# A Mamba-2 scan inside a transformer layer: outputs for pairs of chunks, and the state update beside its own chunk

## The chip, the cores and the metric

The kernel runs on one core of a Trainium2 chip. The metric is the device time of one execution in microseconds (us): the median of three runs before the change is 2607.29 us (2604.95 to 2607.7). The engines that matter are TensorE (PE: matmuls and transposes; its weight loads are listed as PEld), VectorE (DVE), ScalarE (ACT), GpSimd (POOL) and SyncE (SP, which issues most DMAs). Each works through its own instructions in the order in which they stand in the program, and waits on semaphores for the others.

## What is computed

One decoder layer on 1024 tokens of width 1024, in float32: a SwiGLU half, a mixer, a cross-attention to 256 memory tokens, a second SwiGLU half, each with an RMSNorm before and after. The mixer projects the tokens once and gives half of the heads to a stick-breaking attention and half to a Mamba-2 SSD. The change touches the SSD alone. Its core in the reference, cut:

```python
x = xs * dt[..., None]                      # (chunk, 128 tokens, 16 heads, 64)
a_cs = cumsum(dt * a)                       # along the 128 tokens of a chunk
lmat = exp(where(tri, a_cs[l] - a_cs[s], -inf))
cb = einsum('bclgn,bcsgn->bcgls', cc, bc)   # C times B, per group of 8 heads
y_diag = einsum('bcgls,bgrcls,bcsgrp->bclgrp', cb, lmat, x)
states = einsum('bclgn,bgrcl,bclgrp->bcgrpn', bc, exp(a_cs[-1] - a_cs), x)
h = h * exp(a_cs[-1]) + states              # scan over the 8 chunks
y_off = einsum('bclgn,bcgrpn,bgrcl->bclgrp', cc, h_before, exp(a_cs))
y = y_diag + y_off + d_skip * xs            # then gated by silu(z) and normed
```

## The kernel before

Every large product is made of three float32r matmuls on high and low parts of the operands (`mm3`, L275). The work of TensorE is written in one fixed order: each matmul or transpose is chained to the one before it (`_pe`, L101), and so the Python code decides what stands behind what. VectorE and ScalarE get their order from the tile framework's scheduler when the program is built; it is as fixed when the program runs.

The SSD (`ssd`, L1208) runs two generators side by side. `inproj` (L1525) is the filling work: the input projections of the remaining x, B, C and z tiles, three 128x512 matmuls to a step, then the keys of the cross-attention (`keys`, L1498, with 128x256 matmuls). `chunks` (L1419) is the scan. It goes over four quads of four heads, and in each over eight chunks of 128 tokens. `merge` (L157) alternates between the two by the matmul costs that each has used, in the ratio 89000 to 149000; a step of the scan ends at each `yield`.

For a chunk, `early` (L1343) makes what needs no state. On TensorE these are a matmul for the differences of the decay sums (tile `seg`), from the second chunk of a quad on another for the decays from the chunk's start (also a `seg` buffer), and two transposes of x (tile `ms`). ScalarE makes `L` of the first by a Relu (L1356) and an Exp (L1357), and `E` of the second by an Exp (L1364). VectorE makes `xdt` (x times dt, L1371), `M` (L times C B, L1376), `E` times C (L1381) and `xdec` (xdt times the last column of L, L1386). `chunk` (L1391) then has the state matmul (tile `st`, of `xdec`, L1398), the new state `S` on VectorE (L1403, L1406), and eight matmuls into `y` that use 64 columns of the array: four on `M` and, from the second chunk on, four on `S` and `E`. In float32 each of these passes twice, so the profile counts 16. VectorE adds `y` to the skip term (L1413). The loop calls `early` for chunk n+1 and only then `chunk` for chunk n (L1429). `bc` (L1332) makes the C B products and the transposed B, one chunk at a call.

When a quad is done and its z tile exists, `gates` (L1449) multiplies by silu(z), stores the result and adds up squares; `group_norm` (L1475) makes the norm's factors. Behind the merge stand the last gates, the last two keys and the last group norm (L1590 to L1594), then the attention. Silu and Exp do not share a table of ScalarE's, so a table load stands in the program wherever it goes from one to the other.

Of the kernel before, what the change touches and what calls it, by code (L numbers as in the profile page):

```python
# [18 lines left out]
P = 128  # L19
S = 1024  # L20
# [27 lines left out]
class Kern:  # L48
# [1159 lines left out]
    def ssd(self, close):  # L1208

        nc, ap = self.nc, self.ap  # L1210
        with self.tc.tile_pool(name=self.nm("ssa"), bufs=1, reuse_waits="tile") as ep, \
# [120 lines left out]
            def bc(gr, c):  # L1332

                Bt, Ct = env["bc", gr]
                _, cbm, Bl = env["g", gr]
                cs = slice(c * P, (c + 1) * P)
                ps = self.t(pp, [P, 2, P], F32, "seg", bufs=2)
                self.mm(ps[:, 0, :], Bt[:, cs], Ct[:, cs], True, True)
                self.tr(ps[:, 1, :], Bt[:, cs])
                nc.vector.tensor_tensor(out=cbm[:, c, :], in0=ps[:, 0, :], in1=self.tri, op=ALU.mult)  # L1340
                nc.scalar.copy(Bl[:, c, :], ps[:, 1, :])

            def early(qd, c):  # L1343
                hs = slice(4 * qd, 4 * qd + 4)
                xs, (Ct, cbm, Bl), (dt, row, col) = env["x", qd], env["g", qd // 2], env["dt"]

                rb = self.t(sp, [P, 4, P], F32R, "rb", bufs=2)
                nc.vector.tensor_tensor(
                    out=rb, in0=row[:, c, :].bitcast(F32).unsqueeze(1).to_broadcast([P, 4, P]),
                    in1=self.par("sel", 6 + 4 * qd, 4).unsqueeze(2).to_broadcast([P, 4, P]), op=ALU.mult,  # L1350
                )
                seg = self.t(pp, [P, 4, P], F32, "seg", bufs=2)
                self.mm(seg, col[:, c, :], rb, True, True)
                L = self.t(sp, [P, 4, P], F32, "L", bufs=2)

                nc.scalar.activation(L, seg, AF.Relu, scale=-1.0)  # L1356
                nc.scalar.activation(L, L, AF.Exp, scale=-1.0)  # L1357
                E = ed = None
                if c > 0:
                    es = self.t(pp, [P, 4, P], F32, "seg", bufs=2)  # L1360
                    self.mm(es, side, rb, True, True)
                    E = self.t(sp, [P, 4, P], F32, "E", bufs=2)
                    ed = self.t(sp, [P, 4, 1], F32, "ed", bufs=2)
                    nc.scalar.activation(E, es, AF.Exp)  # L1364
# [5 lines left out]
                xdt = self.t(sp, [P, 4, 64], F32, "xdt", bufs=2)  # L1370
# [5 lines left out]
                nc.vector.tensor_tensor(  # L1376
                    out=M, in0=L, in1=cbm[:, c, :].unsqueeze(1).to_broadcast([P, 4, P]), op=ALU.mult
                )
                xdec = None
                if c > 0:  # L1380
                    nc.vector.tensor_tensor(  # L1381
                        out=E, in0=E, in1=Ct[:, cs].unsqueeze(1).to_broadcast([P, 4, P]), op=ALU.mult
                    )
                if c < 7:
                    xdec = self.t(sp, [P, 4, 64], F32, "xdec", bufs=2)
                    nc.vector.tensor_tensor(  # L1386
                        out=xdec, in0=xdt, in1=L[:, :, P - 1 : P].to_broadcast([P, 4, 64]), op=ALU.mult
                    )
                return ed, xdt, M, E, xdec

            def chunk(qd, c, St, ed, xdt, M, CE, xdec):  # L1391
                xs, Bl = env["x", qd], env["g", qd // 2][2]
                cs = slice(c * P, (c + 1) * P)
                yp = self.t(pp, [P, 2, P], F32, "y", bufs=1)
                Sn = None
                if c < 7:
                    sps = self.t(pp, [P, 4, 64], F32, "st", bufs=1)
                    self.mm(sps, Bl[:, c, :], xdec, True, True)  # L1398
                    Sn = self.t(sp, [P, 4, 64], F32, "S", bufs=2)
                    if St is None:  # L1400
                        nc.vector.tensor_copy(Sn, sps)
                    else:
                        nc.vector.tensor_tensor(  # L1403
                            out=Sn, in0=St, in1=ed.to_broadcast([P, 4, 64]), op=ALU.mult
                        )
                        nc.vector.tensor_tensor(out=Sn, in0=Sn, in1=sps, op=ALU.add)  # L1406
                for h in range(4):
                    o = yp[(h % 2) * 64 : (h % 2) * 64 + 64, h // 2, :]
                    self.mm(o, xdt[:, h, :], M[:, h, :], True, St is None)
                    if St is not None:  # L1410
                        self.mm(o, St[:, h, :], CE[:, h, :], False, True)
                for i in range(2):
                    nc.vector.scalar_tensor_tensor(  # L1413
                        out=xs[i][:, cs], in0=xs[i][:, cs], scalar=self.par("d_skip", 2 * qd + i),
                        in1=yp[:, i, :], op0=ALU.mult, op1=ALU.add,
                    )
                return Sn

            def chunks():  # L1419
                env["dt"] = dt_sums(*dt_wide)  # L1420
                yield
                env["g", 0] = env["bc", 0][1], self.t(sp, [P, 8, P], F32, "cbm"), self.t(sp, [P, 8, P], F32, "Bl")
                bc(0, 0)
                yield
                order = [(n // 8, n % 8) for n in range(32)]
                nxt = early(*order[0])
                bc(0, 1)
                yield
                for n, (qd, c) in enumerate(order):  # L1429
                    cur, nxt = nxt, None  # L1430
                    if n < 31:
                        nxt = early(*order[n + 1])
                    St = chunk(qd, c, None if c == 0 else St, *cur)
                    if c == 7:
                        ready.append(qd)
                    gates()
                    if n < 6:
                        bc(0, n + 2)
                    yield
                    if qd == 1 and c > 3:  # L1440

                        env["g", 1] = env["bc", 1][1], *env["g", 0][1:]
                        for i in range(2):
                            bc(1, 2 * (c - 4) + i)
                        yield
# [74 lines left out]
            env = {}  # L1520
# [35 lines left out]
            for i, ti in enumerate((8, 10, 0, 1)):  # L1556
                ps = self.proj_now(next(W), 1)
                if i == 0:
# [6 lines left out]
                    sp = late.enter_context(self.tc.tile_pool(name=self.nm("ssb"), bufs=1, reuse_waits="tile", side="right"))  # L1565
                    pp = late.enter_context(self.tc.tile_pool(name=self.nm("ssps"), bufs=1, reuse_waits="tile", space=PSUM))
# [15 lines left out]
            fill = inproj()  # L1582

            scan = chunks()
            for n in (4, 2, 7):
                for _ in range(n):
                    next(fill)
                if n < 7:
# [807 lines left out]
```

## Time and profile before

| | |
|---|---|
| median of 3 runs | 2607.29 us |
| the profiled execution, span from the first to the last instruction | 2606.7 us |
| busy share: TensorE, weight loads, VectorE, ScalarE, GpSimd | 99%, 82%, 76%, 49%, 22% |
| the scan's matmuls: first seg, last y | 755.5 us, 991.5 us |
| y matmuls (M and S together) | 480 passes, median 0.27 us each as recorded |
| st matmuls | 56 passes for 28 chunks, median 0.38 us as recorded |

The median of the runs is 0.6 us above the profiled execution's span; nothing else lies around it. A matmul's recorded length includes the time in which the next one already streams, so a sum of lengths says little; the distance from one start to the next tells what a matmul costs. In a profile row, `out<-in` are the program's tile names, a number in brackets at the end is idle time before the instruction, with what ended it, and `L1386` is a line of the kernel.

### The profile page before, as it was taken

The numbers are of one execution on the slowest core, as the hardware profiler recorded it, in microseconds if no ns is written. First come the engines' busy times: TensorE is split into PE (matmuls) and PEld (weight loads), VectorE is DVE, ScalarE is ACT, GpSimd is POOL, SyncE is SP. The second block draws the span as 40 slices with busy tenths as digits, with TensorE's granted clock in tenths as the row PEclk, the third lists the DMA queues.
The fourth block names the chain that finished last, engine by engine and source line by source line (L and its number), as shares of the span: only waits on it lengthen the run. The fifth ranks groups of instructions, "written<-read, shape, count | busy, mean of one in ns | idle before, by whom it ended". The sixth has DMA issues, their size and how long they took to land.

```text
span 2606.7 us, 36814 instructions
## 1 busy us (share of the span) xinstructions
PE 2578.2 (99%) x12850; PEld 2148.5 (82%) x12850; DVE 1993.9 (76%) x3044; ACT 1289.7 (49%) x2300; POOL 577.9 (22%) x669
## 2 busy tenths in 40 slices
PE   9999999999999999999999999999999999999999
PEld 7788888888777778888888898888878888888887
DVE  7978987779689884777777777876656888777767
ACT  7434444555356663555555554445554433334543
POOL 2655554001000001111111110101011655551000
PEclk9999999999999999999999999999999999999999
DMA  6468887655656516555555556547558453326554
GB/s 241 158 210 298 300 287 272 209 188 169 224 195 204 182 69 213 162 149 152 141 152 131 169 161 215 206 153 250 196 185 299 146 183 104 109 85 236 184 174 154
DMA packets 216042, 489.82 MB, mean 188 GB/s; under 512 B 26544, under 2 KB 35120, under 8 KB 215856
## 3 DMA queue, kind: packets, MB, share of 16 engines
q1 hardware_dynamic: 169232, 381.02, 44.6%
q0 software_dynamic: 22720, 62.93, 8.1%
q10 hardware_dynamic: 23904, 43.53, 4.5%
q8 instruction: 101, 1.65, 0.3%
q14 instruction: 85, 0.70, 0.1%
HBM read 327.46 MB, written 138.94 MB: 179 GB/s over the span
## 4 chain that ended last, share of the span: by engine, by line
PE 77%; issue 13%; DVE 5%; ACT 1%; DMA 1%; POOL 0%; DVEq 0%; ACTq 0%; POOLq 0%
PE mm L139 38%; PE dn L139 34%; PE z L139 2%; PE tr L142 2%; PE ms L139 1%; PE ms L142 1%; DVE nb L1770 1%; DVE wlo L263 0%; DVE acc L363 0%; DVE hl L263 0%; DVE atl L263 0%; DVE F L1053 0%; DVE xl L263 0%; DVE F L405 0%; DVE xl L417 0%
## 5 line engine op out<-in xcount | busy, mean ns | idle before, releaser
L139 PE MATMUL mm<-xh,whi 128*128 128x512 f32 x1320 | 520.3, 403 | 2.5 <-ACT xh L268 1.1
L139 PE MATMUL mm<-xh,wlo 128*128 128x512 f32 x1272 | 488.7, 391 | 0.0
L139 PE MATMUL mm<-xl,whi 128*128 128x512 f32 (+1 forms) x1252 | 486.9, 389 | 1.8 <-DVE xl L263 1.4
L139 PEld LDWEIGHTS mm<-xh,whi 128*128 128x128 f32 x1320 | 248.2, 188 | 44.6 <-issue 3.8
L139 PEld LDWEIGHTS mm<-xh,wlo 128*128 128x128 f32 x1272 | 238.8, 188 | 52.1 <-DVE wlo L263 0.4
L139 PEld LDWEIGHTS mm<-xl,whi 128*128 128x128 f32 x1252 | 236.1, 189 | 35.9 <-DVE xl L263 2.3
L1770 DVE TENSOR_TENSOR_SCAN nb<-nb,begin 128x128 f32<-128x128 f32 (+7 forms) x128 | 171.3, 1351 | 50.8 <-ACT nb L1766 49.8
L1766 ACT ACTIVATE nb<-z,scale 128x128 f32<-128x128 f32 (+2 forms) x192 | 107.8, 581 | 78.8 <-PE z L139 78.6
L263 DVE TENSOR_TENSOR wlo<-wraw,whi 128x1024 fp32r<-128x1024 f32 x70 | 85.5, 1222 | 54.3 <-ACT whi L261 54.0
L261 ACT CAST whi<-wraw 128x1024 fp32r<-128x1024 f32 (+1 forms) x87 | 84.0, 965 | 78.3 <-PE mm L139 51.1
L658 ACT ACTIVATE ft<-ft 128x512 f32<-128x512 f32 x88 | 55.5, 631 | 99.3 <-DVE ft L657 97.3
L1787 POOL DMA_DIRECT2D mix<-sq x64 | 52.8, 826 | 231.0 <-DVE sq L1785 168.0
L139 PE MATMUL dn<-xh,wlo 128*128 128x512 f32 x296 | 101.3, 390 | 0.0
L757 POOL TENSOR_TENSOR wc<-raw,wraw 128x512 f32<-128x512 f32 x55 | 81.2, 1476 | 57.7 <-DVE blk L263 24.8
L263 DVE TENSOR_TENSOR atl<-tr,ath 128x512 fp32r<-128x512 f32 (+1 forms) x108 | 67.9, 632 | 31.2 <-ACT ath L261 30.8
L757 POOL TENSOR_TENSOR wc<-wraw,raw 128x512 f32<-128x512 f32 x56 | 80.2, 1432 | 50.9 <-DVE whi L263 16.6
L844 POOL TENSOR_TENSOR ft<-ft,e 128x512 f32<-128x512 f32 x37 | 59.7, 1614 | 121.2 <-DVE e L843 45.8
L139 PE MATMUL mm<-ath,v 128*128 128x256 f32 x320 | 85.9, 291 | 0.8 <-ACT sq L1784 0.6
L261 ACT CAST ath<-tr 128x512 fp32r<-128x512 f32 (+1 forms) x108 | 58.9, 546 | 53.3 <-PE tr L142 48.9
L139 PE MATMUL dn<-xh,blk 128*128 128x512 f32 x264 | 85.1, 389 | 0.0
L261 ACT CAST wlo<-wc 128x512 fp32r<-128x512 f32 x79 | 49.1, 621 | 69.9 <-PE dn L139 23.2
L139 PE MATMUL mm<-atl,v 128*128 128x256 f32 x320 | 82.8, 281 | 0.7 <-DVE atl L263 0.7
(579 smaller groups left out, 6775.6 us busy)
## 6 DMA issues: line engine op xcount, KB each, us to landing
whi<-dwhi SPq DMA_DIRECT2D x82, 512.0 KB, 3.6
wlo<-dwlo SPq DMA_DIRECT2D x82, 512.0 KB, 4.7
wraw<-in_w_gu SPq DMA_DIRECT2D x43, 512.0 KB, 4.0
dwhi<-bh SPq DMA_DIRECT2D x78, 256.0 KB, 4.1
dwlo<-bl SPq DMA_DIRECT2D x78, 256.0 KB, 3.9
raw<-in_w_gu SPq DMA_DIRECT2D x37, 512.0 KB, 4.0
wraw<-xs SPq DMA_DIRECT2D x56, 256.0 KB, 3.0
xs<-ft ACTq DMA_DIRECT2D x54, 256.0 KB, 3.7
```

Source lines behind the costliest of these rows:

```text
L139: self._pe(self.nc.tensor.matmul(out, lhsT, rhs, start=start, stop=stop, skip_group_check=self.more), cost)
L142: self._pe(self.nc.tensor.transpose(out, src, self.ident if ident is None else ident), 109.0)
L261: self.kp(self.nc.scalar.copy(hi, src))
L263: self.nc.vector.tensor_tensor(out=lo, in0=src, in1=hi.bitcast(F32), op=ALU.subtract)
L658: nc.scalar.activation(t, t, AF.Silu)
L757: inst = nc.gpsimd.tensor_tensor(out=t, in0=a, in1=b, op=op)
L844: nc.gpsimd.tensor_tensor(out=t1, in0=t1, in1=e, op=ALU.mult)
L1766: nc.scalar.activation(nb[:, s0:s1], z[:, 0:n], AF.Sigmoid, scale=sc[:, i : i + 1])
L1770: nc.vector.tensor_tensor_scan(out=nb[:, 0:Wd][:, ::-1], data0=nb[:, 0:Wd][:, ::-1], data1=begin[:, S - Wd : S][:, ::-1], initial=0.0, op0 ...
L1787: nc.gpsimd.dma_start(out=self.mix_d[p][a * 64 : a * 64 + 64, csl], in_=o, accum_op=ALU.add)
```

## The change

- `early` writes `M` into `L`'s buffer and `E` into one of `rb`'s (both "in place"), makes `xdec` ahead of `M`, and the buffer counts are changed to suit: rb 4, L 3, ed 3, xdt 3, S 3; M and E have no buffers of their own any more.
- `chunk` is split into `state` (the st matmul and the new S) and `outputs` (the y matmuls and the skip term). The loop takes two chunks at a time: `early`, `state`, `early`, `state`, then `outputs` for both, into one `y` tile, with two VectorE instructions on 256 columns instead of four on 128. A `yield` stands between each of these, so that filling work goes there. The call of `early` one chunk ahead is gone.
- `bc` calls are spread over the new steps.
- Eleven steps of projections, not seven, stand ahead of the first chunk.
- The last keys stand ahead of the last gates, and the last group norm's matmuls are pinned 12000 cost units into the attention.

```diff
-                rb = self.t(sp, [P, 4, P], F32R, "rb", bufs=2)
+                rb = self.t(sp, [P, 4, P], F32R, "rb", bufs=4)
...
-                    E = self.t(sp, [P, 4, P], F32, "E", bufs=2)
+                    E = self.t(sp, [P, 4, P], F32, "rb", bufs=4)
...
-                M = self.t(sp, [P, 4, P], F32, "M", bufs=2)
-                nc.vector.tensor_tensor(
-                    out=M, in0=L, in1=cbm[:, c, :].unsqueeze(1).to_broadcast([P, 4, P]), op=ALU.mult
-                )
...
                     xdec = self.t(sp, [P, 4, 64], F32, "xdec", bufs=2)
                     nc.vector.tensor_tensor(
                         out=xdec, in0=xdt, in1=L[:, :, P - 1 : P].to_broadcast([P, 4, 64]), op=ALU.mult
                     )
+                M = L
+                nc.vector.tensor_tensor(
+                    out=M, in0=L, in1=cbm[:, c, :].unsqueeze(1).to_broadcast([P, 4, P]), op=ALU.mult
+                )
...
-            def chunk(qd, c, St, ed, xdt, M, CE, xdec):
...
+            def state(qd, c, St, ed, xdec):
+                if c == 7:
+                    return None
+                Bl = env["g", qd // 2][2]
+                sps = self.t(pp, [P, 4, 64], F32, "st", bufs=1)
+                self.mm(sps, Bl[:, c, :], xdec, True, True)
...
+            def outputs(qd, c, parts):
+
+                xs = env["x", qd]
+                yp = self.t(pp, [P, 2, 2, P], F32, "y", bufs=1)
+                for j, (St, xdt, M, CE) in enumerate(parts):
+                    for h in range(4):
+                        o = yp[(h % 2) * 64 : (h % 2) * 64 + 64, h // 2, j, :]
+                        self.mm(o, xdt[:, h, :], M[:, h, :], True, St is None)
+                        if St is not None:
+                            self.mm(o, St[:, h, :], CE[:, h, :], False, True)
...
-                for n, (qd, c) in enumerate(order):
-                    cur, nxt = nxt, None
-                    if n < 31:
-                        nxt = early(*order[n + 1])
-                    St = chunk(qd, c, None if c == 0 else St, *cur)
...
+                for n in range(16):
+                    qd, c = n // 4, n % 4 * 2
+                    if c == 0:
+                        St = None
+                    parts = []
+                    for j in range(2):
+                        ed, xdt, M, CE, xdec = early(qd, c + j)
+                        if n == 0:
+                            bc(0, 1 + j)
+                        yield
+                        Sn = state(qd, c + j, St, ed, xdec)
+                        parts.append((St, xdt, M, CE))
+                        St = Sn
+                        if n < 3 and 3 + 2 * n + j < 8:
+                            bc(0, 3 + 2 * n + j)
+                        yield
+                    outputs(qd, c, parts)
+                    if c == 6 and qd < 3:
                         ready.append(qd)
                     gates()
...
-            for n in (4, 2, 7):
+            for n in (4, 2, 11):
...
             self.merge(scan, 89000, fill, 149000)
+            self.run_all(keys(6, 8))
             gates()
-            self.run_all(keys(6, 8))
             self.run_later(float("inf"))
-            group_norm(1)
+            with self.pinned(self.clock + 12000):
+                group_norm(1)
```

What this does to the order on TensorE is best seen at one chunk of the first quad. Before, from the last projection matmul ahead of `early` to the first one behind the y matmuls (`mm` is a projection, `csc` and `side` are the two constants of the seg matmuls; the numbers are buffers):

```order
L139 MATMUL mm_7395<-xh_1265_5767,wlo_7219 128x512
L139 MATMUL seg_7420<-rb_7418,csc_7074 128x512
L139 MATMUL seg_7425<-rb_7418,side_6402 128x512
L142 MATMUL ms_7431<-ident_112,xs_6785 128x128
L142 MATMUL ms_7431<-ident_112,xs_6786 128x128
L139 MATMUL st_7442<-xdec_7342,Bl_7102 128x256
L139 MATMUL y_7441<-M_7339,xdt_7337 64x128
L139 MATMUL y_7441<-E_7330,S_7350 64x128
```

The st and y matmuls belong to the chunk before the one whose `early` stands above them: `xdec_7342` and `M_7339` come of an earlier `rb`. In the changed program, an `early` and its `state`:

```order
L139 MATMUL seg_7330<-rb_7328,csc_7074 128x512
L139 MATMUL seg_7335<-rb_7328,side_6402 128x512
L142 MATMUL ms_7341<-ident_112,xs_6785 128x128
L142 MATMUL ms_7341<-ident_112,xs_6786 128x128
L139 MATMUL mm_7323<-xh_1261_5763,whi_7154 128x512
L139 MATMUL mm_7323<-xl_1309_5946,whi_7154 128x512
L139 MATMUL mm_7323<-xh_1261_5763,wlo_7155 128x512
L139 MATMUL st_7355<-xdec_7346,Bl_7102 128x256
```

`xdec_7346` is made of this very chunk's `seg_7330`, and three projection matmuls stand between. Over the 28 chunks that have an st, 3 matmuls stand there in 11, 6 in 15, 9 in one, and 6 of the keys' smaller ones in one. On ScalarE the same stretch of a chunk with a table load reads, in the changed program (`rb_7643` is the tile that was called E):

```order
L1232 ACTIVATE Bt_7479<-Bt_7479 128x1024
L1356 ACTIVATE L_7638<-seg_7636 128x512
L1364 ACT_TABLE_LOAD
L1364 ACTIVATE rb_7643<-seg_7641 128x512
L1357 ACTIVATE L_7638<-L_7638 128x512
```

The load stands between the Relu and the Exps, as it does before the change. There is a load between Relu and the Exp of `L` at 16 of the 28 chunks. And on VectorE in the changed program:

```order
L1371 TENSOR_TENSOR xdt_7509<-ms_7506,dt_6879 128x256
L1348 TENSOR_TENSOR rb_7537<-csr_7073,params_78 128x512
L1386 TENSOR_TENSOR rb_7502<-rb_7502,Ct_6784 128x512
L1378 TENSOR_TENSOR xdec_7511<-xdt_7509,L_7497 128x256
L1401 TENSOR_TENSOR S_7520<-S_7406,ed_7503 128x256
L1382 TENSOR_TENSOR L_7497<-L_7497,cbm_7101 128x512
```

`xdec` (L1378) stands ahead of M (L1382, now `L` itself), which it followed before, and behind `E` times C (L1386).

More of the change, by code (lines that the diff above doesn't have):

```diff
@@ L1369, in early @@
                     self.tr(xp[:, i * P : (i + 1) * P], xs[i][:, cs])
-                xdt = self.t(sp, [P, 4, 64], F32, "xdt", bufs=2)
+                xdt = self.t(sp, [P, 4, 64], F32, "xdt", bufs=3)
                 nc.vector.tensor_tensor(
@@ L1388, in early @@
                     )
-                return ed, xdt, M, E, xdec
-            def chunk(qd, c, St, ed, xdt, M, CE, xdec):
[L1392 to L1411, printed above, removed]
@@ new lines, in early @@
+                M = L
+                nc.vector.tensor_tensor(
+                    out=M, in0=L, in1=cbm[:, c, :].unsqueeze(1).to_broadcast([P, 4, P]), op=ALU.mult
+                )
+                if c > 0:
+                    nc.vector.tensor_tensor(
+                        out=E, in0=E, in1=Ct[:, cs].unsqueeze(1).to_broadcast([P, 4, P]), op=ALU.mult
+                    )
+                return ed, xdt, M, E, xdec
+            def state(qd, c, St, ed, xdec):
[4 more added lines that the diff above has]
+                self.mm(sps, Bl[:, c, :], xdec, True, True)
+                Sn = self.t(sp, [P, 4, 64], F32, "S", bufs=3)
+                if St is None:
+                    nc.vector.tensor_copy(Sn, sps)
+                else:
+                    nc.vector.tensor_tensor(
+                        out=Sn, in0=St, in1=ed.to_broadcast([P, 4, 64]), op=ALU.mult
+                    )
+                    nc.vector.tensor_tensor(out=Sn, in0=Sn, in1=sps, op=ALU.add)
+                return Sn
@@ L1424, in chunks @@
                 yield
[L1425 to L1428, printed above, removed]
[L1429 to L1434 removed]
+                St = None
+                for n in range(16):
+                    qd, c = n // 4, n % 4 * 2
+                    if c == 0:
+                        St = None
+                    parts = []
[12 more added lines that the diff above has]
+                    if c == 6 and qd < 3:
                         ready.append(qd)
                     gates()
[L1437 to L1438 removed]
                     yield
@@ L1442, in chunks @@
                         env["g", 1] = env["bc", 1][1], *env["g", 0][1:]
-                        for i in range(2):
-                            bc(1, 2 * (c - 4) + i)
-                        yield
+                        for i in range(2 * c - 8, 2 * c - 4):
+                            bc(1, i)
+                            if i % 2:
+                                yield
+                ready.append(3)
             ready, yacc = [], []
```

14 lines of the change are left out of this document (5 added, 9 removed).

## The prediction

> **What bounds the kernel now.** I read the page first, then busy time by stretches around the scan, then what TensorE waited for there, and last the rows of single chunks in order of time. The page says that TensorE is never free:
>
> ```profile
> span 2606.7 us, 36814 instructions
> PE 2578.2 (99%) x12850; PEld 2148.5 (82%) x12850; DVE 1993.9 (76%) x3044; ACT 1289.7 (49%) x2300; POOL 577.9 (22%) x669
> ```
>
> The scan and what shares its time run from 745 to 1010 us. Busy time by stretches (length, then busy time of each engine, the granted clock, the DMA share and GB/s):
>
> ```profile
> 745.00:760.00 15.00, 13.61 (x72) 10.84 (x70) 11.34 (x19) 7.41 (x13) 0.00 (x0) 1.00 0.68 231
> 760.00:875.00 115.00, 114.46 (x680) 91.22 (x679) 101.43 (x196) 71.42 (x117) 0.00 (x0) 1.00 0.57 192
> 875.00:995.00 120.00, 120.00 (x778) 98.02 (x777) 99.61 (x205) 78.53 (x130) 0.54 (x1) 1.00 0.34 119
> 995.00:1010.00 15.00, 13.41 (x106) 12.94 (x106) 9.11 (x18) 6.64 (x11) 3.83 (x5) 1.00 0.68 243
> ```
>
> TensorE idles 1.4 + 0.5 + 0.0 + 1.6 = 3.5 us in 265. What it waited for in 740 to 1010 us is the same 3.5 us (total, times, longest):
>
> ```profile
> PE mm L139 <- DVE sq L1511: 1.6, 1, 1.6
> PE seg L139 <- ACT Bl L1341: 1.1, 2, 0.6
> PE seg L139 <- DVE rb L1348: 0.6, 1, 0.6
> PE st L139 <- DVE xdec L1386: 0.2, 1, 0.2
> ```
>
> Every microsecond that TensorE loses here moves the end, and little is left to win by removing waits. Matmul ends are modelled, so I price by distances between starts. One chunk of before on TensorE:
>
> ```profile
> 806.85 0.40 PE L139 MATMUL mm<-xh,wlo 128*128 128x512 f32 x1
> 807.08 0.39 PE L139 MATMUL seg<-rb,csc 128*128 128x512 f32 x1
> 807.31 0.39 PE L139 MATMUL seg<-rb,side 128*128 128x512 f32 x1
> 807.54 0.38 PE L142 MATMUL ms<-ident,xs 128*128 128x128 f32 x2
> 807.76 0.60 PE L139 MATMUL st<-xdec,Bl 128*128 128x256 f32 x2
> 808.28 0.45 PE L139 MATMUL y<-M,xdt 128*64 128x128 f32 x4
> 808.55 0.39 PE L139 MATMUL y<-E,S 128*64 128x128 f32 x4
> 808.77 0.44 PE L139 MATMUL y<-M,xdt 128*64 128x128 f32 x4
> 808.99 0.44 PE L139 MATMUL y<-E,S 128*64 128x128 f32 x4
> 809.36 0.50 PE L139 MATMUL mm<-xh,whi 128*128 128x512 f32 x1
> 809.69 0.40 PE L139 MATMUL mm<-xl,whi 128*128 128x512 f32 x1
> 809.93 0.39 PE L139 MATMUL mm<-xh,wlo 128*128 128x512 f32 x1
> ```
>
> A projection matmul takes 0.23 us, and `early` (two seg, two transposes) 807.08 to 807.76 = 0.68. Four y matmuls take 0.22, but the first four 0.27, the last four until the next projection 0.37, and that one 0.33: each entry into and exit from the 64-column y matmuls costs 0.05 + 0.15 + 0.10, with about 0.1 more ahead of the first (808.28 is 0.52 after two st passes of about 0.22). That is 0.4 us a group.
>
> **The change, part by part.** The same 10013 TensorE rows stand in both programs, so its streaming work is unchanged, and only boundaries and waits count.
>
> *Outputs of two chunks together.* 32 y groups become 16: 16 x 0.4 = 6.4 us gained. VectorE has 34 rows fewer; this is off the path (84% busy, 210 of 250 us), so 0.
>
> *The state behind its own chunk.* Before, the st matmul of a chunk stood behind `early` of the next chunk, a whole interval of some 7 us after its decays were begun. Now it stands 3 or 6 projection matmuls behind its own `early`. Its input xdec needs seg, then Relu and Exp on ScalarE, then a VectorE multiply. How long that takes, from the same chunk on ScalarE, and VectorE's row behind the Exp:
>
> ```profile
> 807.51 0.60 ACT L1356 ACTIVATE L<-seg 128x512 f32<-128x512 f32 x1 [2.67 <-PE seg L139]
> 808.00 0.60 ACT L1364 ACTIVATE E<-seg 128x512 f32<-128x512 f32 x1
> 808.48 0.63 ACT L1357 ACTIVATE L<-L 128x512 f32<-128x512 f32 x1
> 809.14 0.69 DVE L1376 TENSOR_TENSOR M<-L,cbm 128x512 f32<-128x512 f32 x1
> ```
>
> L is ready at 809.11, 2.03 us after seg began. The next row shows the price of xdec and the one place where st had to wait for it:
>
> ```profile
> 759.19 0.42 DVE L1386 TENSOR_TENSOR xdec<-xdt,L 128x256 f32<-128x256 f32 x1
> 759.66 0.70 PE L139 MATMUL st<-xdec,Bl 128*128 128x256 f32 x2 [0.18 <-DVE xdec L1386]
> ```
>
> So xdec is 0.03 + 0.42 + 0.05 more, 2.53; in most chunks E times Ct (0.69 as M) stands ahead of it and holds VectorE until about 0.07 later: **2.6 us** from seg to st. Moving xdec ahead of M, which the change does, is already in this. The cover is 0.68 + 3 x 0.23 = 1.37, or 2.05 behind six. Of the chunks, over half have a table load between Relu and Exp, because Silu runs in between:
>
> ```profile
> 790.70 0.39 PE L139 MATMUL seg<-rb,csc 128*128 128x512 f32 x1
> 791.12 0.60 ACT L1356 ACTIVATE L<-seg 128x512 f32<-128x512 f32 x1 [2.65 <-PE seg L139]
> 791.74 1.28 ACT L1364 ACT_TABLE_LOAD   x1
> 793.53 0.62 ACT L1357 ACTIVATE L<-L 128x512 f32<-128x512 f32 x1
> ```
>
> L ends at 794.15, 3.45 after seg, so st can start **4.0 us** after it. A quad's first chunk has no E and no second seg (early 0.45), and the load:
>
> ```profile
> 814.26 0.39 PE L139 MATMUL seg<-rb,csc 128*128 128x512 f32 x1
> 816.60 0.63 ACT L1357 ACTIVATE L<-L 128x512 f32<-128x512 f32 x1
> ```
>
> 2.97 + 0.5 = 3.5 us, against 1.14 or 1.82. I walked through the changed program's order (TensorE for the cover, ScalarE for the load) for all 28 st:
> - no load, 3 matmuls: 7 x (2.6 - 1.37) = 8.6
> - no load, 6 matmuls: 5 x (2.6 - 2.05) = 2.8
> - load, 6 matmuls: 8 x (4.0 - 2.05) = 15.6
> - load, 3 matmuls, or 6 of the 256-wide ones at the end, which are half as long: 2 x 2.6 = 5.2
> - first chunks of quads 1, 3 (3 matmuls) and 2 (6): 2 x 2.4 + 1.7 = 6.5
> - quad 1, chunk 4: Silu with its own load and then a second load stand between Relu and Exp. That pattern is in the trace once; seg there is 0.42 before Relu as elsewhere:
>
> ```profile
> 875.91 0.60 ACT L1356 ACTIVATE L<-seg 128x512 f32<-128x512 f32 x1 [0.34 <-PE seg L139]
> 878.91 1.28 ACT L1357 ACT_TABLE_LOAD   x1
> 880.20 0.63 ACT L1357 ACTIVATE L<-L 128x512 f32<-128x512 f32 x1
> ```
>
>   880.83 - 875.49 + 0.5 - 1.37 = 4.5
> - quad 0, chunks 0 and 1: loads, 6 and 9 matmuls and two small ones as cover, convolution steps in the queues ahead. Not in the trace; between 0.55 and 2.6 (the rows above), I take 1.9 each, near the six-matmul load case: 3.8
>
> Sum 47 us. While st waits, all projection matmuls behind it wait too, and everything is late by that much: nothing catches up, as TensorE has no idle time to give back later. The bounds: 38 if handoffs, loads and the two unknown chunks come out at their shortest, 56 if each VectorE piece now ahead of xdec (convolution steps, evacuations) delays it.
>
> The Trainium skill's page "ScalarE: Activation LUTs" ("What ACT_TABLE_LOAD costs") gives 2.66 us for each change of set, a load of 1283 ns and a drain of 1380. In this trace the load row is 1.28 and delays Exp by 1.42 in all (3.45 against 2.03). By the page the 16 loads would cost 20 us more, and the sum would be 67; I go by the rows.
>
> *Other parts.* M in L's buffer and E in rb's remove no work: 0; the buffer counts give each at least the reach that a pair needs (if not, rb or L waits for a y group, up to 0.6 as the rb wait above). Four more projection steps ahead of the first chunk, and keys ahead of the last gating, remove at most the 3.5 us of waits above: the rb and Bl waits at the start, and the 1.6 us in which a key matmul waited for its evacuation behind gating work. Against that stands nothing, or a new wait of the keys on their own stores; I take the 3.5. The group norm's place inside attention costs no matmul, and its result is read much later: 0.
>
> Gains 6.4 + 3.5 = 10 us, loss 47: +37. From the profiled execution's 2606.7 us span that is 2643.7; the median of the runs, 2607.29, is 0.6 above the span, so **2644 us**. With the bounds (38 - 11 to 56 - 6): 2634 to 2657.
>
> **Rivals.**
> 1. *Faster.* st doesn't wait, because xdec comes in time; 2607 - 10 = 2597. For it: before, st waited only 0.2 us. Against: then it had 7 us, now 1.4 to 2.05, against a measured 2.03 for Exp alone. It decides below a mean wait of 10 / 28 = 0.36 us a chunk. 0.07.
> 2. *Half covered.* Chunks without a load come in time, since ScalarE runs their Exp ahead of E, and the six-matmul cover holds. Then 11 us fall away: 2633. Against: E stands before the Exp in the program's order. 0.15.
> 3. *VectorE takes over.* Pieces of 1.3 us that queue ahead of xdec, where TensorE's waiting makes evacuations bunch, add 0.5 to 0.7 us to each of 28 chunks: 2658 to 2664. For it: VectorE is 84% busy. 0.08.
> 4. *Level.* Waits and gains balance at 10 us: 2607. 0.03.
>
> One chunk's wait of 4.5 us could cost clock as well. The granted clock is 1.00 in every stretch above, where the longest wait is 1.6 us. By the Trainium skill, "TensorE: Matmul & The Clock Gate" (Part 1), an idle window of some 3.4 us halves the clock until it has been busy for as long, which would by estimate add 2 us or so for this chunk; no row here shows it, and it is not in the sum.
>
> **How the numbers follow.** My forecast has 0.67. I call a change under 0.2% (5 us) the same, about what can be told from none. Faster 0.07 (rival 1), same 0.03, slower 0.90. The main case spans 2634 to 2657; with the half-covered case below and VectorE above, 2620 to 2664 holds the time 8 times in 10.
>
> **What would show it.** Right: st waits for xdec at nearly all 28 chunks, together 40 to 50 us (less up to 0.15 each that modelled ends hide), longest where a load stands between Relu and Exp; the scan lasts some 37 us longer at unchanged DVE busy time; the page's TensorE share falls to about 98%; the 1.6 us wait on sq is gone. y groups: 0.4 us each, 16 of them. Wrong: waits on xdec under 10 us, or stalls that stand at y or seg instead.

## The result and the profile after

The changed kernel takes **2677.83 us** (median of 4 runs, 2676.11 to 2679.17) against 2607.07 for the kernel before, also 4 runs: a ratio of 1.0269, 95% interval 1.0257 to 1.0282. It is slower, as forecast, but by 70.8 us and not by 37; the time lies above the range. The profiled execution's span is 2676.0 us, 69.3 more than before; its time, 2677.79, is 1.8 us above the span, where the prediction added 0.6.

From the page of the changed kernel, the span, TensorE's busy time and the slices of granted clock:

```profile
span 2676.0 us, 36786 instructions
PE 2599.0 (97%) x12850; PEld 2160.3 (81%) x12850; DVE 1994.7 (75%) x3012; ACT 1291.1 (48%) x2300; POOL 578.1 (22%) x669
PEclk9999999999999989999999999999999999999999
```

VectorE's busy time is that of before (1993.9), as the prediction has it, and so is ScalarE's (1289.7). TensorE's share is 97%, where the prediction has 98. What TensorE waited for from 700 to 1100 us (total, times, longest):

```profile
PE st L139 <- DVE xdec L1378: 45.3, 27, 4.8
PE seg L139 <- DVE rb L1348: 2.6, 2, 1.8
PE y L139 <- DVE L L1382: 2.3, 2, 1.2
```

45 us stand at st, at 27 of 28 chunks, and the wait of 1.6 us on sq is gone. The stretches, in the columns of the prediction's second view (length, busy time of each engine, granted clock, DMA share, GB/s); the last y matmul now starts at 1058.0 us:

```profile
760.00:875.00 115.00, 94.40 (x521) 73.05 (x521) 81.14 (x141) 56.85 (x90) 0.00 (x0) 0.96 0.42 143
875.00:1060.00 185.00, 156.83 (x910) 124.35 (x911) 119.01 (x229) 92.91 (x157) 0.54 (x1) 0.92 0.30 104
935.00:1000.00 65.00, 54.34 (x269) 41.39 (x270) 39.63 (x76) 31.02 (x48) 0.00 (x0) 0.84 0.17 61
```

TensorE's idle time in these stretches was to be seen; the granted clock was not: 0.84 in one of 65 us, where before had 1.00 everywhere. One chunk shows both. TensorE's, ScalarE's and VectorE's rows of it:

```profile
974.02 0.39 PE L139 MATMUL seg<-rb,csc 128*128 128x512 f32 x1
975.87 0.40 PE L139 MATMUL mm<-xh,wlo 128*128 128x512 f32 x1
978.07 0.70 PE L139 MATMUL st<-xdec,Bl 128*128 128x256 f32 x2 [1.80 <-DVE xdec L1378]
978.42 0.59 PE L139 MATMUL mm<-xh,whi 128*128 128x512 f32 x1
978.85 0.55 PE L139 MATMUL mm<-xl,whi 128*128 128x512 f32 x1
979.19 0.63 PE L139 MATMUL mm<-xh,wlo 128*128 128x512 f32 x1
979.62 0.63 PE L139 MATMUL seg<-rb,csc 128*128 128x512 f32 x1
```
```profile
974.45 0.60 ACT L1356 ACTIVATE L<-seg 128x512 f32<-128x512 f32 x1 [0.48 <-PE seg L139]
975.07 1.28 ACT L1364 ACT_TABLE_LOAD   x1
976.36 0.60 ACT L1364 ACTIVATE rb<-seg 128x512 f32<-128x512 f32 x1
976.85 0.62 ACT L1357 ACTIVATE L<-L 128x512 f32<-128x512 f32 x1
977.60 0.42 DVE L1378 TENSOR_TENSOR xdec<-xdt,L 128x256 f32<-128x256 f32 x1
```

This chunk's first seg matmul starts at 974.02. Relu, table load, Exp of E and Exp of L end at 977.47, xdec ends at 978.02, and st starts 4.05 us behind seg; the prediction had 4.0 for this class. From 979.19 on matmuls of this size stand 0.43 us apart (979.19 to 979.62) and no longer 0.23: the clock has been halved, after a wait of 1.97 us (2.20 between starts, less the usual 0.23).

**Where 69 us went.** I compare the same 1745 TensorE instructions in both traces, from the first matmul of the decay sums to the first transpose of the attention: 291.2 us before, 358.3 after, +67.1. Each stretch of small matmuls between projections is measured from the start of the last projection ahead to the start of the second behind, less two plain spacings of 0.227 us (0.120 for the keys' 256-wide ones). What a stretch takes over the shortest of its kind is waiting or a halved clock (a kind that occurs once is its own shortest).

| in that part | before | after | difference |
|---|---|---|---|
| small matmuls at their shortest | 83.8 | 79.0 | -4.8 |
| st stretches over their shortest | | 54.5 | +54.5 |
| seg and transposes over their shortest | | 10.1 | +10.1 |
| y over its shortest | | 3.7 | +3.7 |
| all stretches over their shortest | 1.1 | | -1.1 |
| projections and keys over 0.227 and 0.120 | 4.2 | 8.7 | +4.5 |

Between starts, less the usual spacing, the 28 waits at st make 50.1 us. Outside this part the scan begins 1.7 us earlier, and what follows takes 1572.9 us instead of 1569.0. The 1.7 us are no gain of the change: ahead of the scan both programs are the same, and e10 below, which changes nothing there either, begins it 1.3 us earlier. Of the 3.9 us behind, most come of one wait in the attention, before and after:

```profile
PE mm L139 <- ACT sq L1784: 0.6, 1, 0.6
PE mm L139 <- ACT sq L1799: 2.3, 1, 2.3
```

In the changed kernel 3.4 us at half clock follow it, from 1511.40 on. In the other runs this wait lies between 0.7 and 1.8 us; what sets it is not shown.

### The profile page after: what moved, and what is told of

Same layout as the page of the kernel before. It is cut to its first block, busy times and chain, and to the rows that moved or that the text cites. A ratio compares the mean times of both kernels' runs of the same rounds, so it can differ in the third digit from the quotient of the medians.

```text
span 2676.0 us, 36786 instructions
## 1 busy us (share of the span) xinstructions
PE 2599.0 (97%) x12850; PEld 2160.3 (81%) x12850; DVE 1994.7 (75%) x3012; ACT 1291.1 (48%) x2300; POOL 578.1 (22%) x669
## 5 line engine op out<-in xcount | busy, mean ns | idle before, releaser
L139 PE MATMUL mm<-xh,whi 128*128 128x512 f32 x1320 | 531.4, 412 | 1.2 <-ACT xh L268 0.8
L261 ACT CAST ath<-tr 128x512 fp32r<-128x512 f32 (+1 forms) x108 | 58.9, 546 | 53.3 <-PE tr L142 48.7
L139 PE MATMUL dn<-xh,whi 128*128 128x512 f32 x240 | 83.4, 392 | 0.0
```

Of the source, the lines that this page charges most:

```text
L139: self._pe(self.nc.tensor.matmul(out, lhsT, rhs, start=start, stop=stop, skip_group_check=self.more), cost)
L261: self.kp(self.nc.scalar.copy(hi, src))
```

## The experiments

### e1: `early` one chunk ahead again

```diff
+                nxt = early(0, 0)
+                bc(0, 1)
+                yield
 ...
-                        ed, xdt, M, CE, xdec = early(qd, c + j)
+                        (ed, xdt, M, CE, xdec), nxt = nxt, None
+                        if i < 31:
+                            nxt = early(*divmod(i + 1, 8))
```

> The changed kernel, with early called one chunk ahead again (early of chunk c+1, then state of chunk c, then the paired outputs); all else as changed. Theory (the state behind its own chunk costs the time: 50 us of waits of st for xdec, and the slow matmuls after them): waits of st under 2 us in all, granted clock 1.00 through the scan, 16 y groups instead of 32 save 7 us and the shorter start and end waits up to 3, so 2597 us (2592 to 2603), faster than both kernels. Rival (the pairing, the buffers shared by L and M, E and rb, or the longer head cost the time): waits move to y or seg and it stays above 2630.

Measured: 2632.67 us, ratio 1.0095 (1.0078 to 1.0112). TensorE's waits, 740 to 1070 us:

```profile
PE seg L139 <- DVE rb L1348: 10.0, 7, 2.2
PE seg L139 <- ACT L L1356: 4.0, 5, 2.1
PE seg L139 <- ACT bh L209: 3.8, 1, 3.8
PE seg L139 <- ACT ed L1365: 2.0, 3, 0.7
```

No st row is left, and 45 us of the loss are gone: the state's place behind its own chunk is the main cause. But the time isn't 2597. The waits now stand at seg, 20 us in all, with 20 us at half clock. In this order, E of chunk c+2 takes the buffer of E of chunk c, which the outputs of the pair have yet to read; e8 tests that.

### e2: more projections between a chunk and its state

Only the planner's cost of a step is changed, by 500 units (mid, mostly 9 projections) or 1600 (far, 15 to 21 behind one chunk of a pair and 6 to 12 behind the other), so that `merge` puts more filling work between `early` and `state`.

```diff
                             bc(0, 1 + j)
+                        self.clock += 1600
                         yield
                         Sn = state(qd, c + j, St, ed, xdec)
 ...
                         yield
+                        self.clock -= 1600
```

> The changed kernel with a longer distance alone: the scan is charged 500 cost units more between early and state, so mostly 9 projection matmuls stand there instead of 3 or 6 (cover 2.7 us). Theory: chunks without a table load (2.6 us from seg to st) come in time, those with one (4.0) wait 1.3 us each, some 14 to 16 of them: waits about 20 us instead of 50, almost no halved clock, 2597 + 20 = 2617 us (2608 to 2630). Rival (not the distance but the order of the parts costs): within 10 us of 2678.

> As the run with 9 matmuls, but 1600 cost units: 15 to 21 matmuls behind the first early of a pair (cover 4.1 us and more), 6 to 12 behind the second (2.0 to 3.4 us). Theory: first chunks never wait, second ones 0.5 us, or 1.3 with a load: waits 8 to 14 us, 2597 + 11 = 2608 us (2600 to 2618). Rival: within 10 us of 2678.

Measured: 2650.52 us for mid (ratio 1.0163, 1.0148 to 1.0178) and 2635.42 for far (1.0106, 1.0091 to 1.0121). TensorE's waits in mid, then in far:

```profile
PE st L139 <- DVE xdec L1378: 22.4, 18, 3.4
PE seg L139 <- DVE rb L1348: 6.7, 4, 2.9
PE seg L139 <- ACT Bl L1341: 3.1, 2, 1.8
```
```profile
PE st L139 <- DVE xdec L1378: 13.5, 11, 3.5
PE seg L139 <- DVE rb L1348: 4.3, 2, 2.9
PE seg L139 <- ACT Bl L1341: 2.3, 2, 1.2
```

st waits of 45.3 (in after), 22.4 and 13.5 us go with 2677.8, 2650.5 and 2635.4: the loss falls as the cover grows, by more than the waits themselves (31.8 us less of waiting, 42.4 us less of time); the time at half clock in the scan falls too, from 41.0 us to 10.2 in far. Both runs are above what was expected. Part of that stands at seg, whose waits are 10.5 us in mid and 6.6 in far against 2.8 in the changed kernel. A likely reason is that filling work which is moved ahead of st is missing ahead of the next seg; this was not tested by itself.

### e3: the clock kept up

Ahead of 27 of the 28 st, 2 to 39 constant matmuls of 0.12 us (some 43 us in all), sized by the wait at that chunk, into a part of the st bank that nothing else uses. They add work that has no use, and leave every dependence as it is.

```diff
+                for _ in range(FILL[8 * qd + c]):
+                    self._pe(nc.tensor.matmul(both[:, 4:8, :], self.onesr, w, start=True, stop=True), 0.0)
                 self.mm(sps, Bl[:, c, :], xdec, True, True)
```

> The changed kernel with 2 to 39 matmuls of 0.12 us on constants ahead of each st, into an unused half of its bank, as many as just fit into the wait that the trace shows for that chunk (43 us of them in all; they are extra work whose result nothing reads). st starts no later for them, but TensorE is busy meanwhile. Theory (after a wait of some 2 us the granted clock is halved for one or two windows of 3.4 us, and matmuls then stand 0.43 us apart instead of 0.23, about 15 us in all): clock 1.00 through the scan, 2662 us (2657 to 2668). Rival (the slow matmuls come of something that follows the wait itself, as late weights or data, not of idleness): 2678 within 4 us, and spacings of 0.43 us remain.

Measured: 2667.78 us, ratio 1.0225 (1.021 to 1.024); 10 us below the changed kernel, with more work, and at the upper end of the expected range. Stretches as above:

```profile
760.00:875.00 115.00, 109.69 (x682) 90.29 (x681) 82.65 (x142) 58.34 (x93) 0.00 (x0) 1.00 0.44 150
875.00:1050.00 175.00, 166.23 (x1093) 138.85 (x1092) 118.22 (x226) 93.94 (x158) 0.54 (x1) 1.00 0.31 108
```

The clock is 1.00 throughout. In the account above, seg and transposes over their shortest fall from 10.1 to 5.4 us and projections from 8.7 to 2.8, while the y stretches stay (3.9). So the halved clock in the scan cost some 10 us.

### e8 and e9: E's own buffers, and a pair in two pieces

e8 is e1 with buffers for E that no rb shares; e9 also takes away the yields, so that a pair's small matmuls stand in two pieces between projections instead of five.

```diff
-                rb = self.t(sp, [P, 4, P], F32R, "rb", bufs=4)
+                rb = self.t(sp, [P, 4, P], F32R, "rb", bufs=1)
 ...
-                    E = self.t(sp, [P, 4, P], F32, "rb", bufs=4)
+                    E = self.t(sp, [P, 4, P], F32, "E", bufs=3)
 ... e9 only:
-                        yield
                         Sn = state(qd, c + j, St, ed, xdec)
 ...
-                        yield
+                        if j == 0:
+                            yield
```

> The changed kernel with `early` one chunk ahead, as in e1_ahead, but with a buffer of its own for rb and three for E, in place of the common ring of four in which the Exp of E(c+2) had to wait for the outputs of the pair (c, c+1). Theory A (what is left of e1_ahead's excess are the waits of `seg` behind that ring, and the price of cutting a pair's small matmuls into five pieces between projections: by the stretches of after, 2 x 0.93 + 2 x 0.67 + 2.39 = 5.59 us per pair beyond the projections, where before has 2 x 2.63 = 5.27 us): the waits of `seg` fall below 5 us, no halved clock in the scan beyond one or two windows, and 2607 + 16 x 0.32 = 2612 us (2608 to 2618). Theory B (cutting costs nothing, the pair saves 6.4 us as forecast): 2597 to 2603 us. Theory C (the ring is not what held `seg` back): about 2630 us as e1_ahead.

> e8_ring, with `early` of the next chunk, the state of this one and (for the second chunk of a pair) the outputs of both standing in one piece, so that a pair has two pieces between projections, as before, instead of five, and one group of y instead of two. Theory A: 2607 - 16 x 0.26 to 0.4 us = 2601 to 2603 us if nothing waits, 2600 to 2608 in all, 8 to 10 us below e8_ring. Theory B: within 3 us of e8_ring, at 2597 to 2603 us both. Rival to both: the outputs of a pair's second chunk wait for its E and M, since they now have only 9 projections behind their `seg` and the next `early` between: 16 waits of about 1 us, above 2612 us.

Measured: e8 2621.55 us (ratio 1.0054, 1.0042 to 1.0067), e9 2625.16 (1.0067, 1.0054 to 1.0081). The first view is of e8, the second of e9:

```profile
PE seg L139 <- ACT L L1356: 5.1, 6, 2.1
PE seg L139 <- ACT ed L1365: 4.0, 4, 2.0
PE seg L139 <- DVE rb L1348: 2.8, 2, 2.1
```
```profile
PE seg L139 <- ACT L L1356: 5.1, 6, 2.1
PE seg L139 <- ACT ed L1365: 4.4, 4, 2.4
PE seg L139 <- DVE rb L1348: 3.5, 2, 2.9
```

The common ring was a true cause in e1: the waits for rb fall from 10.0 to 2.8 us and the time by 11. Theory C falls. **Theory A falls too**: e9 isn't 8 to 10 us below e8 but 3.6 above it, with overlapping runs. The figures of theory A were miscounted. The stretches ran to the third projection behind and so held three plain spacings, of which I took off two; with the third taken off five pieces, and not two, the changed order is cheaper: before 2 x 2.40 = 4.80 us a pair, after 2 x 0.69 + 2 x 0.45 + 2.16 = 4.44. Cutting costs nothing. Theory B's 2597 fails as well, because of what still waits: all rows of this view come to 15 us in e8 and 17 in e9, against 3.5 before, most of it behind ScalarE's L and ed. I read this so: the pieces of one pair stand close together (6 to 9 projections in e9), and `seg` and `bc` share two PSUM buffers that ScalarE must empty. But a good part stands at the first chunks alone. From 740 to 800 us e9 has:

```profile
PE seg L139 <- ACT L L1356: 4.9, 5, 2.1
PE seg L139 <- ACT Bl L1341: 1.8, 1, 1.8
```

That is nearly all of its waits for L and Bl. The next experiment shows another reason for waits at this place.

### e67 and e10: the ends alone, the masked decays alone

e67 is the kernel before with 11 steps ahead of the first chunk and the changed end (last keys ahead of the last gates, group norm pinned). e10 is the kernel before with M in L's place, xdec made ahead of it:

```diff
-                L = self.t(sp, [P, 4, P], F32, "L", bufs=2)
+                L = self.t(sp, [P, 4, P], F32, "L", bufs=3)
 ...
-                M = self.t(sp, [P, 4, P], F32, "M", bufs=2)
+                M = L
```

> The kernel before with only the two edits outside the scan's loop: 11 steps of projections ahead of the first chunk in place of 7, and the last keys ahead of the last gating with the group norm pinned. Theory A (they are worth what the prediction gave them, nothing to 3.5 us of gain): 2603 to 2608 us, and the wait of 1.6 us on sq behind the scan gone. Rival (the ends hold part of the loss: in the changed kernel what follows the scan took 3.9 us more): 2610 to 2612 us.

> The kernel before with only the masked decays in place: M written over L (three buffers), xdec's product ahead of M's. Theory A (no engine that matters waits for them): 2605 to 2609 us. Rival (a product written over its own input, or the longer life of L, holds VectorE or ScalarE back until PE waits): above 2611 us, with new PE waits on L or rb in the scan.

Measured: e67 2614.56 us (ratio 1.0025, 1.0014 to 1.0036), e10 2606.79 (0.9997, 0.9989 to 1.0006). Masks in place cost nothing, as predicted. The ends alone cost 7 us, more than either side had expected, and mostly not where the rival put it: behind the scan e67 takes 1570.4 us against 1569.0. It is the first chunk. TensorE, ScalarE and VectorE of e67:

```profile
764.72 1.22 PE L139 MATMUL st<-xdec,Bl 128*128 128x256 f32 x2 [3.90 <-DVE xdec L1386]
```
```profile
758.04 1.24 ACT L1220 ACTIVATE xs<-u,params 128x1024 f32<-128x1024 f32 x1 [2.09 <-DVE u L1217]
759.19 0.57 ACT L1356 ACTIVATE L<-seg 128x512 f32<-128x512 f32 x1
761.26 1.28 DVE L1225 SCALAR_TENSOR_TENSOR xs<-u,params,xs 128x1022 f32<-128x1022 f32 x1
763.05 1.28 DVE L1225 SCALAR_TENSOR_TENSOR xs<-u,params,xs 128x1023 f32<-128x1023 f32 x1
764.25 0.42 DVE L1386 TENSOR_TENSOR xdec<-xdt,L 128x256 f32<-128x256 f32 x1
```

In before this xdec started at 759.19 and st waited 0.18 us (rows in the prediction). Four steps more bring a projection's convolution (1.24 on ScalarE ahead of Relu, pieces of 1.28 on VectorE between Exp and xdec) into the first chunk's chain. The wait of 3.9 us is followed by 6.8 us at half clock, from 763.71 on.

### e5: the changed kernel with 7 steps ahead

```diff
-            for n in (4, 2, 11):
+            for n in (4, 2, 7):
...
-                if n < 11:
+                if n < 7:
```

> The changed kernel with 7 steps of projections ahead of the first chunk in place of 11; all else as changed. Theory H (the four steps more bring a projection's convolution, 1.25 us on ACT and 3 x 1.28 us on DVE, in front of the first chunk's Relu, Exp and xdec, as in e67_ends, whose first chunk waited 3.9 us for xdec and whose clock was then halved for 6.8 us): 4 to 7 us below the changed kernel, 2671 to 2674 us. Rival (in the changed kernel the first chunks wait for their own chain in any case, and the convolution hides in that wait, or only moves to the next chunk): within 2 us of it, 2676 to 2680 us.

Measured: 2677.85 us, ratio 1.0271 (1.0257 to 1.0285): no difference from the changed kernel. Theory H falls, and the rival holds. What costs 7 us in the order of before is covered in the changed one, whose chunks wait for their own chain anyway (48.7 us at st in all, against 50.1).

### e11, e13, e14: pairing with an even spacing

e11 is e9 with 7 steps ahead and a planner's cost that puts 15 to 24 projections behind each of a pair's two pieces. e13 gives rb its second buffer; room comes from xdec and two small tiles. e14 is e13 with the end of before.

```diff
                         if j == 0:
+                            self.clock += 1700
                             yield
+                            self.clock -= 1700
 ... e13:
-                rb = self.t(sp, [P, 4, P], F32R, "rb", bufs=1)
+                rb = self.t(sp, [P, 4, P], F32R, "rb", bufs=2)
 ...
-                    xdec = self.t(sp, [P, 4, 64], F32, "xdec", bufs=2)
+                    xdec = self.t(sp, [P, 4, 64], F32, "xdec", bufs=1)
```

> e9_joined with two things changed: 7 steps of projections ahead of the first chunk as in the kernel before, and some 1700 of the planner's units between a pair's two pieces, so that 15 to 24 projections stand behind each piece (in e9_joined 6 to 9 behind the first and 30 to 39 behind the second). Theory D (pairing is worth about what the prediction gave it; beyond the stretches' shortest times, e8_ring and e9_joined lost it to waits of `seg` and of the transposes for ACT, because two pieces stood close together with only two PSUM buffers named seg, and to the head; the pieces of one pair cost 2 x 2.39 = 4.78 us net in before, and 2 x 0.69 + 2 x 0.44 + 2.15 = 4.41 us in after): 2607.5 - 16 x 0.37 - 1.6 for the wait on sq = 2600 us (2598 to 2604). Theory A, as it was put for e8_ring (the cutting or the joining sets what the small matmuls cost, not the waits) has no loss left to name here and would also have 2601 to 2603; what would speak against D is a time above 2606, or waits of seg above 4 us in the scan at such a spacing.

> e11_even with two buffers for rb in place of one; the room for it is taken from xdec (one in place of two) and from the two small tiles of the split dt*A, which now lie where csr and csc come later. Theory D': what e11_even still gave back, 6 us of waits of `seg` for rb and a halved clock of 3.4 us, comes from rb's single buffer, which puts its product on DVE late, behind the sums of the chunk before (in before, with two buffers, rb of the next chunk stood done 8 us ahead). Then the waits of seg for rb fall to about 1 us, and with the 4 to 6 us that pairing saves the time is 2600 to 2604 us. Rival (rb is late because VectorE is full of other work at those places: convolutions of 3 x 1.28 us and the gating; or xdec's single buffer now makes st wait): within 2 us of e11_even, 2607 to 2611 us.

> e13_rb2 with the end of the stage as in the kernel before (last gating ahead of the last keys, group norm not pinned). Theory T (the changed end removes the wait of 1.6 us of the projections on sq, and gives 1 to 1.8 us back behind the scan, as the spans of e67_ends and e11_even behind it showed): within 1.5 us of e13_rb2. Rival (the changed end is worth the 1.6 to 3 us that were put on it): 1.6 to 3 us above e13_rb2.

Measured: e11 2609.26 us (ratio 1.0004, 0.9995 to 1.0013), e13 **2605.14** (0.9991, 0.9982 to 1.0), e14 2607.21 (0.9998, 0.9989 to 1.0007). Waits of e11, then of e13:

```profile
PE seg L139 <- DVE rb L1348: 5.2, 5, 2.3
PE seg L139 <- ACT L L1356: 1.2, 5, 0.2
```
```profile
PE seg L139 <- DVE rb L1348: 1.6, 2, 1.0
PE seg L139 <- ACT L L1356: 1.2, 5, 0.2
```

Theory D's mechanism holds in part. The waits of e9 for ed (4.4 us) and of y for S (1.7), which stand behind 800 us, are gone with the even spacing. The waits for L and Bl at the first chunks (6.7 us) have fallen to 1.8, but there e11 also has four steps of projections less, so how much of that is the spacing is not shown. D's time of 2598 to 2604 doesn't hold, for a wait on rb remains. A second buffer for rb removes 3.6 us of it and 4.1 us of time, as D' has it, though the time is 1 us above its range. e13's part of 1745 instructions takes 286.6 us against 291.2 before; 0.9 of the 4.6 is given back behind it. Its median is 2.7 us below before's, at the edge of what can be told from none, and it is the lowest here. e14 stands 2.1 us above e13, as its rival has it, but with overlapping runs: whether the changed end is worth that stays open. With the end of before, pairing gains 0.7 us in the median, which can't be told from none.

## Why the prediction was right and wrong

| term | forecast | measured |
|---|---|---|
| waits at st | +47 | +50.1 between starts, +54.5 by stretches |
| halved clock in the scan | 0 in the sum | +10 (e3) |
| new waits at seg, transposes and y, less those of before | 0 | +8 (5.4 and 3.7, less 1.1) |
| pairing | -6.4 | -4.8 in all, 0.36 us a pair |
| sq gone; ahead of and behind the scan | -3.5 | -1.4, -1.7, +3.9 |

In the order 54.5 + 10.6 + 5.4 + 3.7 - 1.1 - 4.8 - 1.4 - 1.7 + 3.9 this is 69.1 us of the 69.3 between the spans, with 10.6 the clock's share by the account of e3. Of the 32 us above the forecast of +37, the clock has 10.6, the new waits 8.0, st 7.5, the ends 4.3 and pairing 1.6.

- **The mechanism was right.** st waits for xdec of its own chunk at nearly every chunk, and e1, which moves `early` ahead again, takes 45 us back. Two of the prices held: 4.05 us from seg to st with a load, 4.0 forecast, and 3.48 at a quad's first chunk (836.97 to 840.45), 3.5 forecast. Without a load it is mostly 2.90 (921.71 to 924.60) and not 2.6, since VectorE's product for the next rb (0.68 us) stands ahead of E times Ct there. The Trainium skill's page "ScalarE: Activation LUTs" ("What ACT_TABLE_LOAD costs") would have made the sum 67 with 2.66 us a load; the 50 measured side with the row of 1.28 us.
- **The failed step is the clock**, put as "One chunk's wait of 4.5 us could cost clock as well", about 2 us and outside the sum; it cost some 10 us (e3). I looked at the longest wait and asked whether it fills 3.4 us. Waits from 1.9 us on did it, where enough of them fell into one window (last section): at nine places in the scan, with 41 us at half clock, and once behind it. It is the largest of the terms that were missing, and not the only one: e3, with the clock at 1.00, still takes 2667.78 us, above the range.
- **A second step failed with it: "only boundaries and waits count" was followed for one wait alone.** "The buffer counts give each at least the reach that a pair needs" and costing the other parts at 0 left out that other work moves together with st: new waits stand at seg (for rb) and at y (for L), 8 us in all. At the longest wait of seg for rb (1.76 us, until 939.03), VectorE comes to that rb only at 938.20, after work without a pause from 933.26 on: the last piece of a convolution, xdec and what follows it. That TensorE's stops pushed this work together is argued and was not tested. Rival 3 had this cause, "where TensorE's waiting makes evacuations bunch", but put it at xdec.
- **Pairing** was sized nearly right (5.8 us at 0.36 a pair, 6.4 forecast; 4.8 in the sum of all stretches, whose single kinds hold some waits of before). As a gain in time it is hardly shown: e13 and e14 lie 2.7 and 0.7 us below before.
- **The ends** gave 1.4 us, the wait on sq, and not 3.5. "Against that stands nothing" missed the convolution in front of the first chunk, which costs time in the order of before (e67), though none that can be seen in the changed one (e5), and the longer wait in the attention.
- M in L's buffer at 0 was right (e10). E in rb's buffer was not tried alone in the changed order; in the order of e1 the common ring cost 11 us (e8). VectorE has 32 rows fewer (3044 to 3012), not 34. Rivals 1, 2 and 4 are excluded by the 45 us at st, at 27 of 28 chunks.

## What to carry to other kernels

When work is moved behind its own producers, price the chain from the rows and the cover from the order; that gave the sign, and 50 of the 69 us. Then price what the stalls do: a TensorE that stood still for more than 2 us of a window of 3.4 us mostly ran the next window at half clock, and there are new waits elsewhere. Grouping small matmuls depends on where the pieces stand and on which buffers they share: 73 us lie between the changed kernel and e13, which pair the same chunks, and even e13 is only at the edge of a gain.

## What the runs showed of the hardware that was not expected

**The clock is halved in whole windows of 3.413 us on a fixed grid, and a window that is partly idle is enough.** In the changed kernel the halved windows begin at 760.47, 780.95, 876.52 us and so on, apart by whole multiples of 3.413. Windows of that grid (columns as before; the clock stands behind the five busy times), each halved one under the one ahead of it:

```profile
897.00:900.41 3.41, 0.95 (x5) 0.48 (x5) 2.27 (x5) 2.68 (x5) 0.00 (x0) 1.00 0.65 225
900.41:903.83 3.42, 3.42 (x10) 2.64 (x11) 1.14 (x3) 0.76 (x2) 0.00 (x0) 0.50 0.00 0
975.57:978.98 3.41, 1.61 (x8) 1.02 (x7) 2.95 (x7) 1.96 (x4) 0.00 (x0) 0.99 0.29 111
978.98:982.34 3.36, 3.36 (x11) 2.58 (x10) 1.51 (x4) 1.67 (x4) 0.00 (x0) 0.50 0.00 0
801.43:804.84 3.41, 2.06 (x13) 1.43 (x11) 2.84 (x7) 1.67 (x4) 0.00 (x0) 1.00 0.78 299
804.84:808.26 3.42, 3.42 (x18) 2.61 (x16) 2.49 (x6) 3.18 (x6) 0.00 (x0) 1.00 0.02 5
```

TensorE was busy for 0.95 and 1.61 us ahead of the halved windows, and for 2.06 ahead of one at full clock. Counted over the scans of nine kernels that had halved windows (after, e1, both e2, e5, e67, e8, e9, e11), with idle time taken from the distances between starts: of the windows at full clock from the first matmul of the decay sums to the last y, all 22 with at least 2.4 us idle were followed by a halved one, 13 of 16 with 2.05 to 2.4, and none of 652 with less. So one wait of 2.4 us that falls into one window cost the next 3.4 us half their speed, and from 2.05 on most did. Shorter waits add up: in e1 two of 1.27 and 0.93 us in one window (from 866.90 on) were followed by a halved one. A wait across a window's edge cost no clock: in e9 one of 3.05 us (from 911.97 on) lay 1.45 us in one window and 1.60 in the next, and none was halved. That this share decides is read from the traces; it was not tried by moving a wait against the grid.

The Trainium skill's page "TensorE: Matmul & The Clock Gate" (Part 1) speaks of a free-running window of 4096 cycles and of an idle window of some 3.4 us. The grid agrees with the first. On the second the measurement decides: some 60% of a window idle was enough here.
